# Moving a sum of weights ahead of its operand, and three operand loads ahead of a store, in the second MLP product of an encoder block

## The chip, the cores and the metric

The kernel runs on one core of one Trainium2 chip. The metric is the device time of one execution in microseconds (us), the median over several runs. A core has TensorE (PE, matrix products), VectorE (DVE), ScalarE (ACT), GpSimd (POOL) and SyncE (SP, which here issues the DMAs). Each engine works through its own queue in order; semaphores join them.

## The reference, cut to what matters

One layer of an encoder over 1024 tokens with 1024 channels: attention and a short convolution, gated and merged, then the squared-ReLU MLP that this change lies in:

```python
h = rms_norm(x, norm2_g) @ w_mlp_in          # 1024 -> 4096
x = x + jnp.square(jax.nn.relu(h)) @ w_mlp_out   # 4096 -> 1024
```

Inputs and outputs are float32.

## The kernel before, in words

Float32 products are made from float16 pairs: each operand is scaled by a power of two and split into a high and a low half (the high half by ACT, the low half by VectorE as the scaled value less the high half), and three of the four products of halves are summed (`PASSES`). Large products are also done by a scheme of Strassen's kind: the matrices are cut into 2 x 2 blocks, and seven products of sums of blocks take the place of eight.

**First MLP product.** It runs in 16 quads, `q` = 0 to 15 (`quad`, `seven`). A quad has seven units of 12 matmuls, in the order 1, 6, 5, 4, 2, 7, 3, with an evacuation ("post") for each: `post5`, `post7` (L1298 to L1300) and `post3` (L1303) on VectorE, and others on L1295, L1307, L1308 and L1310. When a quad is done, `h_done(q)` lets ACT take the ReLU and the square (L1269, L1271), lets POOL make the sums of blocks (L1138) and stores all seven forms to HBM, in `HS[q // 4]` (L1275, on SP). So HS[0] holds quads 0 to 3, and HS[3] is complete with quad 15.

**Second MLP product.** It sums over four sections `s` of the hidden channels. A section has seven products `o` = 0 to 6 in the order of `ORDER`: w11, t2, w21, t3, t1, t4, w22. That is 28 groups, n = 7 s + o, of four units each (`j`, one for every 128 tokens of a block); a unit is 12 matmuls and fills one bank. Weights of the section are `w11`, `w12` (four raw tiles) and `w21`, `w22` (tile w2x); sums of them are made in place by POOL: after w11's operand is ready, w11 becomes t1 = w11 + w12 (L1403) and t2 = w11 + w12 + w22 is written to a tile of its own (L1404); after t2's, w12 becomes w12 + w22 = t3 (L1408); after t3's, t2 takes up w21 and so becomes t4 (L1412).

`prep2(s)` prepares a section's operands. It squares the weights on ACT into a scratch tile, keeping only the sums of squares (L1357, L1360); from these it gets a scale, through a column sum on VectorE and TensorE (`sum_of`, L924, and `scale_of`, which waits for three units of matmuls). Then for each group it scales and splits the activations (ACT L1388, VectorE L1390) and the weights (ACT L1393, VectorE L1397, two halves each) into the tile `OPS[16 + n]`. These tiles rotate through three buffers (`TAGS`), and `gate(i)` holds a group back until TensorE's instructions of two groups ahead of it have been issued; the buffer itself comes free when TensorE has read it. Activations come back from HS by `h_load(n)` (L1343) into one of four slots of the tile `hf`, slot n % 4. Two are loaded apart: n = 0 into half of the tile h0 (L1426), and n = 1 into that half of `OPS[17]` where its weights will later stand (L1368). So L1393 of n = 1 can write only when L1390 of n = 1 has read. For section 0 the other half of h0 is first the scratch for squares and then the tile of t2; later sections have the tiles `junk` and `t2`.

The order of instructions is made by generators. Each `unit` emits its matmuls, then the post of the unit ahead (`settle`), and then lets foreground generators take `steps` steps and the first background generator (`prep2` at the end of the kernel) `ticks` ticks up to its next `yield`. So where a `yield` stands sets the place of an instruction in its engine's queue. During quad 15, n = 0's and n = 1's operands are prepared between its posts. `hf` lies in the buffer of u2T, the activations of the first product, so `h_load(2)` comes after quad 15; `h_load(3)` is issued when all stores of sums have been issued:

```python
    h_load(2)
    settle()
    while live:
        step()
    h_load(3)
```

After that, group n issues `h_load(n + 2)`. Posts of the second product add a bank into `acc` (ACT L1487 for s = 0, VectorE L1489 later) or straight into the residual `X1` (VectorE L1498). In the last section `combine` (L1460 to L1469) adds the accumulators on POOL and VectorE, and finished rows are stored.

Of the kernel before, what the change touches and what calls it, by code (L numbers as in the profile page):

```python
# [11 lines left out]
F16 = mybir.dt.float16  # L12
BF16 = mybir.dt.bfloat16
I32 = mybir.dt.int32
AF = mybir.ActivationFunctionType
OP = mybir.AluOpType
# [36 lines left out]
def encoder_block(ctx: ExitStack, tc: tile.TileContext, x, weights, cols, gqk, rel, masks, out):  # L53
    nc = tc.nc
    V, A, G, T, SP = nc.vector, nc.scalar, nc.gpsimd, nc.tensor, nc.sync
# [27 lines left out]
    def cols_of(kind, n):  # L83
        a = area[kind]
        if a[1] + n > a[2]:
            assert kind != "keep"
            a[1] = a[0]
        a[1] += n
        return slice(a[1] - n, a[1])

    def keep(n=1):
        return cols_of("keep", n)
# [4 lines left out]
    def at(c, i, n=1):  # L97
        return slice(c.start + i, c.start + i + n)

    def mul(a, b, out=None):  # L100
        out = out or tmp(a.stop - a.start)
        V.tensor_tensor(sc[:, out], sc[:, a], sc[:, b], op=OP.mult)
        return out
# [23 lines left out]
    def step(n=1):  # L127
        for _ in range(n):
            for g in list(fg):
                if not advance(g):  # L130
                    fg.remove(g)
# [42 lines left out]
    def ones_col():  # L174
        turn[0] = (turn[0] + 1) % 4
        return ones[:, 128 + turn[0]:129 + turn[0]]
# [23 lines left out]
    def settle():  # L200
        while late:
            late.pop(0)()
# [9 lines left out]
    def load_upto(n):  # L212
        while loaded[0] < min(n, len(loads)):
            ch, p = loads[loaded[0]]
            loaded[0] += 1
            t = rawp.tile([128, 1024], F32, name="raw")
            load_into(t[:, :ch.widths[p][0] * ch.widths[p][1]], ch, p)
            ch.raw.append(t)
# [637 lines left out]
    for k in range(N + 11):  # L856
        p, w = k // 16, k % 16
# [63 lines left out]
    def sum_of(sm):  # L921

        b, a = cols_of("prep", 1), ones_col()
        V.tensor_reduce(sc[:, b], sc[:, sm], axis=AX, op=OP.add)  # L924
        V.tensor_copy(a, sc[:, b])
        return a, work[0]

    def scale_of(am, more, n=3):

        a, mark = am  # L930
        yield from apart(mark, n * 6144, work)
        b, s, inv = cols_of("prep", 1), cols_of("prep", 1), keep()
        yield from all_sum(a, b, anybank(), 1e-36)
        yield from pow2_half(b, 14, s, inv, more)
        return s, inv
# [239 lines left out]
    TAGS = ((base2, "B"), (base, "K"), (base, "V"))  # L1175
    tsum = {}

    def gate(i):
        while pe_done[0] < i - 2 or (i == 2 and pair_done[0] < 4):
            yield  # L1180
# [54 lines left out]
    def wait(n):  # L1235
        for _ in range(n):
            yield
# [93 lines left out]
    OPS, X2 = {}, {}  # L1331
    later = {}

    def w2x_load(s):
        pool = later["pool"] if s == 1 else wsp
        X2[s] = pool.tile([128, 4, 1024], F32, name="w2x", tag="w2x" if s == 1 else "ws", bufs=1 if s == 1 else 2)
        for i in range(4):
            load_into(X2[s][:, i], c2x[s], i)

    def h_load(n):  # L1340
        s, f = n // 7, ORDER[n % 7][0]
        later["h", n] = later["hf"][:, n % 4]
        SP.dma_start(later["h", n], HS[s][:, f])  # L1343
# [3 lines left out]
    def prep2(s):  # L1347
        raw, x2 = c2[s].raw, X2[s]
        w11, w12 = raw[0:2], raw[2:4]
        w21, w22 = [x2[:, i] for i in range(2)], [x2[:, i] for i in range(2, 4)]  # L1350
        while not r_ready[s]:
            yield
        Rs, iR = R[s]
        sm = cols_of("prep", 6)
        j = later["junk"]
        for i in range(4):
            A.activation(j[:, :1024], raw[i], AF.Square, scale=sc[:, iR], accum_out=sc[:, at(sm, i)])  # L1357
            yield
        for i in range(2):
            A.activation(j, x2[:, 2 * i:2 * i + 2].rearrange("p a c -> p (a c)"), AF.Square, scale=sc[:, iR],  # L1360
                         accum_out=sc[:, at(sm, 4 + i)])
            yield
        sums = sum_of(sm)
        if s == 0:
            yield from gate(17)
            P = OPS[17] = TAGS[17 % 3][0].tile([128, 2, 2, 2048], F16, name="ops", tag=TAGS[17 % 3][1])
            later["h", 1] = P[:, 0].rearrange("p w m -> p (w m)").bitcast(F32).rearrange("p (k t) -> p k t", k=4)
            SP.dma_start(later["h", 1], HS[0][:, ORDER[1][0]])  # L1368
        sw, inv = yield from scale_of(sums, 0)
        fw = keep()  # L1370
        mul(iR, sw, fw)
        c2[s].inv = inv
        yield
        T2 = None
        for o, (f, name) in enumerate(ORDER):
            n = 7 * s + o
            i = 16 + n
            yield from gate(i)
            pool, tag = TAGS[i % 3]
            if n != 1:  # L1380
                OPS[i] = pool.tile([128, 2, 2, 2048], F16, name="ops", tag=tag)
            P = OPS[i]
            while ("h", n) not in later:
                yield
            if 1 < n < 26:
                h_load(n + 2)
            hf = later.pop(("h", n)).rearrange("p k t -> p (k t)")
            A.activation(P[:, 1, 0], hf, AF.Copy, scale=sc[:, Rs])  # L1388
            yield
            V.scalar_tensor_tensor(P[:, 1, 1], hf, sc[:, Rs], P[:, 1, 0], op0=OP.mult, op1=OP.subtract)  # L1390
            w = {"w11": w11, "t1": w11, "t3": w12, "w21": w21, "w22": w22}.get(name) or [T2[:, i] for i in range(2)]
            for i2 in range(2):
                A.activation(P[:, 0, 0, 1024 * i2:1024 * i2 + 1024], w[i2], AF.Copy, scale=sc[:, fw])  # L1393
            yield
            for i2 in range(2):
                sl = slice(1024 * i2, 1024 * i2 + 1024)
                V.scalar_tensor_tensor(P[:, 0, 1, sl], w[i2], sc[:, fw], P[:, 0, 0, sl], op0=OP.mult, op1=OP.subtract)  # L1397
                yield
            ready.add(i)
            if name == "w11":  # L1400
                T2 = later["t2"]()
                for i2 in range(2):
                    G.tensor_tensor(w11[i2], w11[i2], w12[i2], op=OP.add)  # L1403
                    G.tensor_tensor(T2[:, i2], w11[i2], w22[i2], op=OP.add)  # L1404
                    yield
            elif name == "t2":
                for i2 in range(2):
                    G.tensor_tensor(w12[i2], w12[i2], w22[i2], op=OP.add)  # L1408
                yield
            elif name == "t3":  # L1410
                for i2 in range(2):
                    G.tensor_tensor(T2[:, i2], T2[:, i2], w21[i2], op=OP.add)  # L1412
                yield
            elif name == "t1":
                done[0] += 4
                load_upto(done[0] + 5)
                if s < 3:
                    w2x_load(s + 1)
                    bg.append(prep2(s + 1))
            yield  # L1420

    def first2():
        h0 = wsp.tile([128, 2, 4, 512], F32, name="h0", tag="ws")
        w2x_load(0)
        later["h", 0] = h0[:, 0]
        SP.dma_start(h0[:, 0], HS[0][:, 0])  # L1426
        later["t2"] = lambda: h0[:, 1].rearrange("p (a k) t -> p a (k t)", a=2)
        later["junk"] = h0[:, 1].rearrange("p k t -> p (k t)").bitcast(BF16)[:, :2048]
        yield from wait(12)

    bg.append(first2())
    bg.append(prep2(0))
    whole(14)
    whole(15)


    later["hf"] = base.tile([128, 4, 4, 512], F32, name="hf", tag="U")
    h_load(2)
    settle()
    while live:  # L1440
        step()
    h_load(3)
    p4.close()
    p5 = ExitStack()
    w5p = later["pool"] = p5.enter_context(tc.tile_pool(name="p5", bufs=1, reuse_waits="tile"))
# [1 line left out]
    t2 = w5p.tile([128, 2, 1024], F32, name="t2")  # L1447
# [25 lines left out]
    for n in range(28):  # L1473
        s, o = n // 7, n % 7
# [92 lines left out]
```

## Time and profile before

| | |
|---|---|
| median of 3 runs | 1295.95 us (1295.22 to 1296.48) |
| the profiled execution, own time | 1298.12 us |
| its span, first to last instruction | 1296.0 us |
| granted TensorE clock over the span | 0.981 of full |
| busy: PE / DVE / ACT / POOL | 94% / 73% / 59% / 33% |
| second MLP product on TensorE | from 976.9 us to the end |

Times in the profile are us from the start of the span. A line such as L1397 is a line of the kernel. In a timeline a row gives the start, the length, the engine, the line, the operation, output <- input, shape and count; a bracket at its end holds the idle time of the engine just before it and what ended that idle time. Matmuls are pipelined, so a unit's row is a little longer than the distance to the next one.

### The profile page before, as it was taken

The numbers are of one execution on the slowest core, as the hardware profiler recorded it, in microseconds if no ns is written. First come the engines' busy times: TensorE is split into PE (matmuls) and PEld (weight loads), VectorE is DVE, ScalarE is ACT, GpSimd is POOL, SyncE is SP. The second block draws the span as 40 slices with busy tenths as digits, with TensorE's granted clock in tenths as the row PEclk, the third lists the DMA queues.
The fourth block names the chain that finished last, engine by engine and source line by source line (L and its number), as shares of the span: only waits on it lengthen the run. The fifth ranks groups of instructions, "written<-read, shape, count | busy, mean of one in ns | idle before, by whom it ended". The sixth has DMA issues, their size and how long they took to land. (4 is left out here: it accounts for less than half of the span.)

```text
span 1296.0 us, 17018 instructions
## 1 busy us (share of the span) xinstructions
PE 1217.8 (94%) x6294; PEld 579.5 (45%) x6294; DVE 940.0 (73%) x1719; ACT 763.9 (59%) x1169; POOL 433.7 (33%) x269
## 2 busy tenths in 40 slices
PE   5999997889999999999997899999996899999998
PEld 4544443444444444444456444444442344444443
DVE  7578767878657686886575476667746588889798
ACT  6777557667564455533665678777774564646430
POOL 2430011111231111100102587667738316080562
PEclk8999999989999999999998999999998899999999
DMA  6558445646552221225284454445462762526112
GB/s 251 125 196 159 106 70 118 132 81 139 113 112 84 65 65 37 70 86 193 63 165 104 147 179 140 151 157 179 170 228 90 240 239 92 234 98 244 67 64 98
DMA packets 170803, 173.35 MB, mean 134 GB/s; under 512 B 131424, under 2 KB 131936, under 8 KB 166624
## 3 DMA queue, kind: packets, MB, share of 16 engines
q1 hardware_dynamic: 170720, 172.27, 44.8%
q8 instruction: 49, 0.80, 0.3%
q14 instruction: 34, 0.28, 0.1%
HBM read 102.51 MB, written 37.75 MB: 108 GB/s over the span
## 5 line engine op out<-in xcount | busy, mean ns | idle before, releaser
L188 PEld LDWEIGHTS <-w 128*128 128x128 f16 x1512 | 149.7, 100 | 161.8 <-issue 9.8
L188 PEld LDWEIGHTS <-ops 128*128 128x128 f16 x1356 | 133.5, 99 | 181.3 <-issue 26.7
L1138 POOL TENSOR_TENSOR as<-as 128x512 f32<-128x512 f32 x64 | 111.7, 1746 | 85.3 <-ACT as L1271 81.6
L854 PE MATMUL ps_d<-uT,w_ws 128*128 128x512 f16 x528 | 128.3, 384 | 2.5 <-ACT w_ws L290 2.4
L188 PE MATMUL ps_s<-ops 128*128 128x512 f16 (+1 forms) x528 | 121.3, 380 | 7.1 <-ACT acc L1487 4.2
L188 PE MATMUL ps_d<-ops 128*128 128x512 f16 x492 | 115.4, 385 | 9.7 <-DVE as L1298 9.7
L188 PEld LDWEIGHTS <-uT 128*128 128x128 f16 x648 | 64.7, 100 | 70.7 <-issue 5.9
L1388 ACT ACTIVATE ops<-hf,sc 128x2048 f16<-128x2048 f32 x26 | 51.8, 1994 | 69.7 <-PE ps_d L188 24.7
L188 PE MATMUL ps_d<-u2T,w 128*128 128x512 f16 (+1 forms) x420 | 89.4, 365 | 3.3 <-DMA u2T<-v 2.9
L971 DVE SCALAR_TENSOR_TENSOR w<-raw,sc,w 128x512 f16<-128x512 f32 (+1 forms) x32 | 40.7, 1272 | 67.7 <-ACT w L977 67.7
L188 PEld LDWEIGHTS <-w_s 128*128 128x128 f16 x588 | 56.7, 98 | 71.3 <-DMA uT<-gs 2.2
L188 PE MATMUL ps_s<-u2x,w 128*128 128x512 f16 (+1 forms) x396 | 85.1, 366 | 3.2 <-DMA u2x<-v 3.2
L1390 DVE SCALAR_TENSOR_TENSOR ops<-hf,sc,ops 128x2048 f16<-128x2048 f32 x26 | 70.7, 2718 | 16.0 <-ACT ops L1388 16.0
L944 ACT ACTIVATE raw<-raw,sc 128x256 f32<-128x256 f32 x184 | 76.0, 494 | 6.1 <-DMA raw<-in_weights 6.1
L188 PE MATMUL ps_o<-ops 128*128 128x512 f16 x336 | 77.5, 380 | 1.4 <-DVE ops L1397 0.8
L958 POOL TENSOR_TENSOR tsum<-raw 128x512 f32<-128x512 f32 x30 | 50.8, 1710 | 81.2 <-ACT raw L944 66.3
L854 PEld LDWEIGHTS <-w_ws 128*128 128x128 f16 x528 | 51.1, 99 | 58.3 <-issue 3.9
L1403 POOL TENSOR_TENSOR raw<-raw 128x1024 f32<-128x1024 f32 x8 | 22.7, 2837 | 140.8 <-DVE ops L1397 140.8
L1269 ACT ACTIVATE as<-as 128x2048 f32<-128x2048 f32 x16 | 30.5, 1909 | 62.9 <-DVE as L1303 62.9
L958 POOL TENSOR_TENSOR gsum<-raw 128x512 f32<-128x512 f32 x14 | 18.5, 1338 | 133.4 <-issue 68.7
L971 DVE SCALAR_TENSOR_TENSOR w<-tsum,sc,w 128x1024 f16<-128x1024 f32 x30 | 61.4, 2087 | 0.0
L278 DVE SCALAR_TENSOR_TENSOR w_ws<-raw,sc,w_ws 128x512 f16<-128x512 f32 (+2 forms) x72 | 51.1, 764 | 3.5 <-ACT w_ws L290 3.5
(300 smaller groups left out, 2526.4 us busy)
## 6 DMA issues: line engine op xcount, KB each, us to landing
raw<-in_weights SPq DMA_DIRECT2D x92, 512.0 KB, 4.0
hs<-as SPq DMA_DIRECT2D x16, 1792.0 KB, 6.9
hf<-hs SPq DMA_DIRECT2D x26, 1024.0 KB, 10.4
w2x<-in_weights SPq DMA_DIRECT2D x16, 512.0 KB, 6.8
raw<-in_weights SPq DMA_DIRECT2D x16, 384.0 KB, 4.0
xt<-in_x SPq DMA_DIRECT2D x8, 512.0 KB, 9.8
gs<-s SPq DMA_DIRECT2D x4, 1024.0 KB, 6.6
x<-in_x SPq DMA_DIRECT2D x8, 512.0 KB, 8.6
```

Source lines behind the costliest of these rows:

```text
L188: T.matmul(ps, l, r, start=a, stop=b)
L278: V.scalar_tensor_tensor(lo, self.raw[p][:, o:o + m], sc[:, c:c + 1], hi, op0=OP.mult, op1=OP.subtract)
L854: T.matmul(ps, l, r, start=a, stop=b)
L944: A.activation(v, v, AF.Copy, scale=sc[:, at(g, 4 * i + k)])
L958: G.tensor_tensor(t[:, o], a, b, op=OP.add)
L971: V.scalar_tensor_tensor(P[:, a:b, 1], w, sc[:, s], P[:, a:b, 0], op0=OP.mult, op1=OP.subtract)
L1138: sub.tensor_tensor(z[o], z[a], z[b], op=op)
L1269: A.activation(f[:, 0:4], f[:, 0:4], AF.Relu)
L1388: A.activation(P[:, 1, 0], hf, AF.Copy, scale=sc[:, Rs])
L1390: V.scalar_tensor_tensor(P[:, 1, 1], hf, sc[:, Rs], P[:, 1, 0], op0=OP.mult, op1=OP.subtract)
L1403: G.tensor_tensor(w11[i2], w11[i2], w12[i2], op=OP.add)
```

## The change

In section 0 the scratch for the squares is no longer half of h0 but part of `OPS[16]`, the operand tile of n = 0, which is therefore taken earlier (behind `gate(16)`). In all sections t2 is made on POOL right behind the squares, as w12 + w22 and then + w11, which are four POOL additions; behind w11's operand only the two that make t1 remain. The yields there change with it: one behind the new additions, one behind t1's instead of two. `h_load(2)`, `h_load(3)` and `h_load(4)` are issued together ahead of the last store of sums, and group n issues `h_load(n + 3)` instead of `h_load(n + 2)`.

```diff
@@ prep2
-        j = later["junk"]
+        if s == 0:
+            yield from gate(16)
+            OPS[16] = TAGS[16 % 3][0].tile([128, 2, 2, 2048], F16, name="ops", tag=TAGS[16 % 3][1])
+            j = OPS[16][:, 0, 0].bitcast(BF16)
+        else:
+            j = later["junk"]
...
         sums = sum_of(sm)
+        T2 = later["t2"]()
+        for i in range(2):
+            G.tensor_tensor(T2[:, i], w12[i], w22[i], op=OP.add)
+            G.tensor_tensor(T2[:, i], T2[:, i], w11[i], op=OP.add)
+        yield
...
-        T2 = None
...
-            if n != 1:
+            if n > 1:
                 OPS[i] = pool.tile([128, 2, 2, 2048], F16, name="ops", tag=tag)
...
-            if 1 < n < 26:
-                h_load(n + 2)
+            if 1 < n < 25:
+                h_load(n + 3)
...
             if name == "w11":
-                T2 = later["t2"]()
                 for i2 in range(2):
                     G.tensor_tensor(w11[i2], w11[i2], w12[i2], op=OP.add)
-                    G.tensor_tensor(T2[:, i2], w11[i2], w22[i2], op=OP.add)
-                    yield
+                yield
@@ first2
-        later["junk"] = h0[:, 1].rearrange("p k t -> p (k t)").bitcast(BF16)[:, :2048]
@@ behind quad 15
-    h_load(2)
+    for n in (2, 3, 4):
+        h_load(n)
     settle()
     while live:
         step()
-    h_load(3)
```

## The prediction

> **What bounds the kernel now.** I read the page first, then TensorE's timeline from the first unit of the second MLP product (group n = 0, where its operands are named ops) to the end, and behind each gap the other engines' timelines and the waits.
>
> ```profile
> span 1296.0 us, 17018 instructions
> PE 1217.8 (94%) x6294; PEld 579.5 (45%) x6294; DVE 940.0 (73%) x1719; ACT 763.9 (59%) x1169; POOL 433.7 (33%) x269
> ```
>
> TensorE is busy 94% of the span, so a change to the preparation of operands can only be worth what TensorE idles, or runs at a low clock, in the stage it touches. All edits lie in that product, so the gaps there are the whole budget.
>
> ```profile
> 976.86 1.73 PE L188 MATMUL ps_o<-ops 128*128 128x512 f16 x7
> ...
> 980.41 2.75 PE L188 MATMUL ps_d<-ops 128*128 128x512 f16 x12
> 983.00 2.75 PE L188 MATMUL ps_s<-ops 128*128 128x512 f16 x12
> ...
> 995.48 5.28 PE L188 MATMUL ps_d<-ops 128*128 128x512 f16 x12 [9.72 <-DVE as L1298]
> 1003.48 2.75 PE L188 MATMUL ps_o<-ops 128*128 128x512 f16 x12
> ...
> 1019.02 2.75 PE L188 MATMUL ps_d<-ops 128*128 128x512 f16 x12
> 1025.94 0.59 PE L188 MATMUL ps_s<-ops 128*128 128x512 f16 x1 [4.16 <-ACT acc L1487]
> ...
> 1034.33 2.75 PE L188 MATMUL ps_d<-ops 128*128 128x512 f16 x12
> ...
> 1092.10 2.75 PE L188 MATMUL ps_o<-ops 128*128 128x512 f16 x12 [0.60 <-DVE acc L1489]
> ...
> 1258.73 2.75 PE L188 MATMUL ps_s<-ops 128*128 128x512 f16 x12 [0.47 <-DVE x L1498]
> ...
> 1281.67 2.75 PE L188 MATMUL ps_s<-ops 128*128 128x512 f16 x12 [2.06 <-DVE x L1498]
> ...
> 1289.44 2.78 PE L188 MATMUL ps_s<-ops 128*128 128x256 f16 x24
> ```
>
> Each row is one unit of 12 matmuls: start, length, and in brackets the idle time before it with its releaser. Three undisturbed units separate the last two rows: 7.77 / 3 = 2.59 us a unit. The 112 units (28 groups of 4) would take 290.1; from 976.86 to 1289.44 + 2.59 they take 315.2. So 25.1 us are lost, and the rows hold nearly all of it:
> - start of n = 0: 980.41 - 976.86 - 2.59 = 0.96;
> - first large gap, with the slow units after it: 1003.48 - 983.00 - 3 x 2.59 = 12.7 (9.9 of gap, 2.8 of low clock);
> - second large gap: 1034.33 - 1019.02 - 3 x 2.59 = 7.5;
> - the three late ones: 0.60 + 0.47 + 2.06 = 3.1.
>
> The other 0.8 I leave alone.
>
> **The first gap** is told by three engines together.
>
> ```profile
> 969.93 8.28 POOL L1138 TENSOR_TENSOR as<-as 128x512 f32<-128x512 f32 x4 [17.48 <-ACT as L1271]
> ...
> 988.24 3.20 POOL L1404 TENSOR_TENSOR h<-raw,w2x 128x1024 f32<-128x1024 f32 x1
> ...
> 991.47 1.15 ACT L1393 ACTIVATE ops<-h,sc 128x1024 f16<-128x1024 f32 x1 [4.43 <-POOL h L1404]
> ...
> 979.21 4.43 DVE L1390 SCALAR_TENSOR_TENSOR ops<-ops,sc 128x2048 f16<-128x2048 f32 x1
> ...
> 987.07 2.17 DVE L1397 SCALAR_TENSOR_TENSOR ops<-h,sc,ops 128x1024 f16<-128x1024 f32 x1 [2.83 <-ACT ops L1393]
> 992.65 2.17 DVE L1397 SCALAR_TENSOR_TENSOR ops<-h,sc,ops 128x1024 f16<-128x1024 f32 x1 [3.41 <-ACT ops L1393]
> 994.75 0.68 DVE L1298 TENSOR_TENSOR as<-ps_d,as 128x512 f32<-128x512 f32 x1
> ```
>
> POOL finishes t2 (tile h) only at 991.4: it first does the sums of quad 14, then adds w11 and t2 in turn. ACT's copy for n = 1 waits, VectorE's L1397 waits behind it, and behind L1397 in VectorE's queue stands L1298, which reads the bank that TensorE needs for the fourth unit of n = 0. So TensorE restarts at 995.48.
>
> **Edit 1, t2 behind the squares.** It takes two POOL adds a section from behind w11's operand and puts four ahead (two adds for each of two halves): two more a section. POOL idles 17.48 us before 969.93. t2's buffer is not a scratch for squares any more (n = 0's own tile is) and w12, w22 are all it needs. A 128x1024 add takes:
>
> ```profile
> L1403 POOL TENSOR_TENSOR raw<-raw x8: 2342/2838/3329, 978.2 to 1216.8; 128x1024 f32<-128x1024 f32 x8
> w2x<-in_weights SPq DMA_DIRECT2D x4, 512.0 KB, 5.7
> 949.57 1.88 SPq L210 DMA_DIRECT2D w2x<-in_weights  x4
> ```
>
> The last w2x is issued at about 951.0 and lands 5.7 later, 956.7. Four adds of 2.34 to 3.33 end at 966 to 970, hidden in the idle stretch. If they run late, the sums of quad 14 are queued behind them (due 967 to 970), and behind these the store and the loads.
>
> The new scratch tile also lets the squares start sooner.
>
> ```profile
> 947.04 2.18 ACT L977 ACTIVATE w<-tsum,sc 128x1024 f16<-128x1024 f32 x2
> 953.57 1.15 ACT L1357 ACTIVATE h<-raw,sc 128x1024 bf16<-128x1024 f32 x1 [4.35 <-DVE w L971]
> 958.66 2.00 ACT L1360 ACTIVATE h<-w2x,sc 128x2048 bf16<-128x2048 f32 x1
> 962.92 0.16 DVE L924 TENSOR_REDUCE sc<-sc 128x1 f32<-128x6 f32 x1 [7.39 <-ACT h L1360]
> ```
>
> ACT waited 4.35 for VectorE to leave that buffer. The new scratch lies in a buffer that quad 13 read last, two quads earlier, so ACT can begin at 949.3, do the four raw squares in 5.1 and the w2x pair (4.2) when it has landed, about 955.7: end near 960 instead of 962.9. I take 2.5 us earlier (bounds 0, if landing is late, and 4.35). VectorE stood 7.39 us at L924, with quad 14's posts queued behind it, so its whole queue moves.
>
> New course: L1390 of n = 1 started at 979.21, right behind n = 0's last L1397; it now starts at 976.7, so n = 0 is ready when TensorE asks for it at 976.86 (0.96 saved). At 4.43, as POOL will again be adding, it ends at 981.1; its f32 source lies where L1393 writes, so ACT waits for it, then copies the first half, 1.15; L1397 2.17, L1310 (a PSUM post like L1298, now between the halves, since w11 yields once less) 0.68, L1397 2.17, L1298 0.68: 988.0. TensorE wanted its bank at 985.59, so 2.4 of 9.9 us remain. Fast ends (L1390 2.35, L1397 1.27, in the rows below) give 984.2: no gap; with no advance it is 990.5, a gap of 4.9, with low clock at up to 2.8.
>
> ```profile
> L1390 DVE SCALAR_TENSOR_TENSOR ops<-hf,sc,ops x26: 2332/2352/3789, 1003.3 to 1274.5; 128x2048 f16<-128x2048 f32 x26
> L1397 DVE SCALAR_TENSOR_TENSOR ops<-raw,sc,ops x24: 1268/1277/2301, 974.8 to 1256.7; 128x1024 f16<-128x1024 f32 x24
> 668.00 2.53 PE L188 MATMUL ps_o<-u2T,w 128*128 128x256 f16 x12
> ```
>
> A gap of 2.06 at 1281.67 left the next units at full speed. The row at 668.00, behind a gap of 2.1, took 2.53 for 12 matmuls of 256 columns where the row at 1289.44 has 24 of them in 2.78, so low clock after 2.4 is possible; I take none, keeping 2.8 for the range. [...]
>
> Next late: the operand of n = 2. Quad 15's ACT passes stand before it. L1298 and three posts like it run from 987.3, 0.68 each: 990.0. Then come two ACT passes over 2048 elements and L1388, 2.0 each (the row at 1021.24 below has 2.00), L1390 at 3.0 (an estimate between its 2.35 and 3.79) and two L1397 at 2.17: 1003.3. TensorE is at n = 2 at 988.0 + 12.95 = 1001.0 and needs the second weight half 1.3 later: a wait of 1.0. First gap in all: 12.7 - 2.4 - 1.0 = 9.3 saved.
>
> **Edit 2, loads three ahead.**
>
> ```profile
> hs<-as SPq DMA_DIRECT2D x16, 1792.0 KB, 6.9
> hf<-hs SPq DMA_DIRECT2D x26, 1024.0 KB, 10.4
> ...
> 1009.62 0.53 SPq L1275 DMA_DIRECT2D hs<-as  x1
> ...
> 1021.24 2.00 ACT L1388 ACTIVATE ops<-hf,sc 128x2048 f16<-128x2048 f32 x1 [13.55 <-DMA hf<-hs]
> ```
>
> n = 3's load stood on SP behind the last store, which waits for POOL's sums; it went out behind that store's issue (1009.62 + 0.53) and landed 11 us later, while ACT waited 13.55 and kept the accumulator copies behind it, hence TensorE. Now loads 2, 3, 4 go out behind quad 14's store, at 969.93 + 8.28 - 2.5 = 975.7: 1.8 + 3 x 1.05 MB. They also wait for the buffer of u2T, which quad 15 reads last; TensorE leaves that quad at 976.86. At what the DMA moved when full
>
> ```profile
> 954.00:968.00 14.00, 13.63 (x65) 6.17 (x63) 4.22 (x9) 10.88 (x14) 0.00 (x0) 1.00 1.02 357
> ```
>
> (357 GB/s) that is 14 us: all landed at 991. L1388 wants n = 2 at 994 and n = 3 at about 1000. The last store is behind them on SP and is read only by the fourth section. In steady state a load still waits for its buffer's L1390, four buffers as before: no change. Saved 7.5; if the loads share so badly that n = 3 comes 13 later, 0.
>
> **Edit 3, later sections.** The same t2 wait sits there.
>
> ```profile
> ACT ops L1393 <- POOL t L1404: 36.8, 6, 7.8
> DVE ops L1397 <- ACT ops L1393: 24.8, 8, 3.4
> 1232.48 0.74 DVE L1489 SCALAR_TENSOR_TENSOR acc<-ps_s,sc,acc 128x512 f32<-128x512 f32 x1
> ```
>
> ACT waits 36.8 us for t2 in the three later sections, up to 7.8 at a time. VectorE's row is for all four sections, 24.8 / 8 = 3.1 before each half, 6.2 a section; it then works off sums 13 us late (n = 21's first bank was full at 1258.09 - 16 x 2.59 + 2.59 = 1219.2). That lag causes the 0.60 and, carried on, the 0.47 and 2.06. With t2 ready some 7 us sooner they go: 3.1 (bounds 0 and 3.1).
>
> The sum: 0.96 + 9.3 + 7.5 + 3.1 = 20.9. The profiled execution took 1298.1, its span 1296.0 and 2.1 around it; it becomes 1277.2, and the median of the runs, 2.2 below it, becomes **1275.0**.
>
> **Rivals.**
> B: VectorE's queue beside POOL takes the first gap over: no advance, gap 4.9 plus 2.8 low clock, and half of the late 3.1 kept: 1275.0 + 5.3 + 1.5 = 1282. For it: POOL adds all through 967 to 988.
> C: VectorE is quick there; no gap is left: 1275.0 - 3.4 - 0.8 = 1271.
> D, slower: eight more adds beside VectorE make it the bound. L1390 stretches from 2.35 to 3.79 and L1397 from 1.28 to 2.30 beside POOL, 3.5 us a group. It decides once TensorE waits 7 us more in each of three later sections, the 20.9 over three. Against: VectorE's busy time was 203.0 of 250 us from 1000 to 1250,
>
> ```profile
> 1000.00:1250.00 250.00, 244.86 (x1120) 109.91 (x1119) 202.98 (x196) 134.91 (x124) 101.71 (x36) 0.98 0.43 161
> ```
>
> and gives up the waits for t2. Price at three stretched groups a section: 3 x (10.4 - 7) = 10 over the old time, 1306. [...]
> E: the loads don't help, since bandwidth or ACT's queue keeps n = 3 late: 1275.0 + 7.5 = 1282.5.
>
> **How the numbers follow.** Forecast 0.60, B 0.18, C 0.12, E 0.06, D 0.04. The range runs from 1270.5 (all 25.1 gone, with 0.3 to spare) to 1283, past B and E; 0.2% is 2.6 us, about what a measurement can tell from no change. All but D are faster, even B, E and all of the late 3.1 together (1275.0 + 5.3 + 7.5 + 3.1 = 1291). D in part ends within the bound: faster 0.96, same 0.01, slower 0.03.
>
> **What the profile will show.** Right: POOL adds into h at 956 to 970; ACT's L1393 of n = 1 no longer names POOL; the 9.72 gap shrinks to about 2.4, its releaser still VectorE; ACT never waits for hf; no gap at 1281. Wrong: a gap over 5 us in n = 0 to 2, hf still a releaser, or VectorE gaps behind POOL at the section starts.

## The result, and the profile after

The changed kernel takes 1279.22 us (median of 4 runs, 1277.69 to 1281.09), the kernel before 1296.22 on the same chip (4 runs). The ratio is 0.9867, 95% interval 0.9849 to 0.9886. The profiled execution took 1279.16 us, its span is 1277.0. In the new source L1388 has become L1397, L1390 L1399, L1393 L1402, L1397 L1406, L1487 L1493, L1489 L1495 and L1498 L1504; the additions for t2 are L1371 and L1372.

TensorE's timeline of the second product, as before:

```profile
975.49 2.75 PE L188 MATMUL ps_o<-ops 128*128 128x512 f16 x12
...
980.67 2.75 PE L188 MATMUL ps_s<-ops 128*128 128x512 f16 x12
987.75 5.28 PE L188 MATMUL ps_d<-ops 128*128 128x512 f16 x12 [4.32 <-DVE as L1298]
992.82 3.21 PE L188 MATMUL ps_s<-ops 128*128 128x512 f16 x12
995.87 2.75 PE L188 MATMUL ps_o<-ops 128*128 128x512 f16 x12
...
1270.48 2.78 PE L188 MATMUL ps_s<-ops 128*128 128x256 f16 x24
```

One gap is left. From 975.49 to 1270.48 + 2.59 the 112 units take 297.6 us, 7.5 more than 112 x 2.59 where it was 25.1 before. Nearly all of the 7.5 is this gap and the slow units behind it: 987.75 - 980.67 - 2.59 = 4.5, and 995.87 - 987.75 - 2 x 2.59 = 2.9. So 17.6 us went inside the product. Another 1.4 lies ahead of it (it begins at 975.49 instead of 976.86): 0.4 is the wait at 963.91, which is gone, and most of the rest (0.9) was already there when quad 14 began, ahead of everything that the change touches. Together that is the span's 19.0. The medians of the runs differ by 17.0 only, since the profiled execution of before lies 1.9 us above its median (1298.12 against 1296.22) and that of the changed kernel lies on its own median.

POOL, ACT and VectorE around the gap that is left (each engine's timeline):

```profile
956.11 2.35 POOL L1371 TENSOR_TENSOR h<-raw,w2x 128x1024 f32<-128x1024 f32 x1 [4.51 <-issue]
...
963.30 2.35 POOL L1372 TENSOR_TENSOR h<-h,raw 128x1024 f32<-128x1024 f32 x1
966.50 7.38 POOL L1138 TENSOR_TENSOR as<-as 128x512 f32<-128x512 f32 x4 [0.85 <-ACT as L1271]
975.05 7.68 POOL L1411 TENSOR_TENSOR raw<-raw 128x1024 f32<-128x1024 f32 x2 [1.17 <-DVE ops L1406]
982.69 6.61 POOL L1415 TENSOR_TENSOR raw<-raw,w2x 128x1024 f32<-128x1024 f32 x2
...
980.61 2.19 ACT L1402 ACTIVATE ops<-h,sc 128x1024 f16<-128x1024 f32 x2 [6.01 <-DVE ops L1399]
...
976.09 4.43 DVE L1399 SCALAR_TENSOR_TENSOR ops<-ops,sc 128x2048 f16<-128x2048 f32 x1
981.79 2.02 DVE L1406 SCALAR_TENSOR_TENSOR ops<-h,sc,ops 128x1024 f16<-128x1024 f32 x1 [1.28 <-ACT ops L1402]
...
984.34 2.76 DVE L1406 SCALAR_TENSOR_TENSOR ops<-h,sc,ops 128x1024 f16<-128x1024 f32 x1
987.02 0.68 DVE L1298 TENSOR_TENSOR as<-ps_d,as 128x512 f32<-128x512 f32 x1
```

t2 is finished at 965.65, in POOL's idle stretch, at 2.35 an addition. ACT's copy for n = 1 no longer waits for POOL but for VectorE's L1399, whose float32 source lies where the copy writes. L1399 takes 4.43 and the two halves of L1406 2.02 and 2.76, while POOL makes t1 (L1411, 975.05 to 982.7) and then t3 (L1415) beside them.

The loads, on SP and at ACT's activation scaling of n = 3, which waited 13.55 us before and now has no bracket:

```profile
974.52 3.02 SPq L1343 DMA_DIRECT2D hf<-hs  x3
...
999.84 2.00 ACT L1397 ACTIVATE ops<-hf,sc 128x2048 f16<-128x2048 f32 x1
```

In the last section VectorE adds n = 21's first bank at 1211.77. TensorE had filled it at 1270.48 - 27 x 2.59 + 2.59 = 1203.1, so VectorE is 8.6 us behind where it was 13 before. The gaps at n = 9, 25 and 27 are gone.

```profile
1211.77 0.74 DVE L1495 SCALAR_TENSOR_TENSOR acc<-ps_s,sc,acc 128x512 f32<-128x512 f32 x1
```

### The profile page after: what moved, and what is told of

Same layout as the page of the kernel before. It is cut to its first block, busy times and chain, and to the rows that moved or that the text cites. A ratio compares the mean times of both kernels' runs of the same rounds, so it can differ in the third digit from the quotient of the medians.

```text
span 1277.0 us, 17035 instructions
## 1 busy us (share of the span) xinstructions
PE 1214.9 (95%) x6294; PEld 578.5 (45%) x6294; DVE 961.3 (75%) x1719; ACT 763.7 (60%) x1169; POOL 463.0 (36%) x277
## 4 chain that ended last, share of the span: by engine, by line
PE 66%; DVE 15%; ACT 8%; DMA 5%; issue 4%; POOL 2%; SPq 1%; DVEq 0%; ACTq 0%; POOLq 0%
PE ps_d L188 24%; PE ps_s L188 22%; PE ps_o L188 14%; PE ps_d L854 5%; DMA PT<-P 2%; DMA hs<-as 2%; DVE w_s L971 1%; DVE w_ws L278 1%; ACT w L977 1%; POOL sform L480 1%; PE ps_s L778 1%; PE ps_o L835 1%; DVE sz L792 1%; DVE sc L301 1%; ACT raw L944 1%
## 5 line engine op out<-in xcount | busy, mean ns | idle before, releaser
L188 PE MATMUL ps_s<-ops 128*128 128x512 f16 (+1 forms) x528 | 118.7, 375 | 0.0
L1397 ACT ACTIVATE ops<-hf,sc 128x2048 f16<-128x2048 f32 x26 | 52.0, 1999 | 95.1 <-PE ps_d L188 39.9
L1399 DVE SCALAR_TENSOR_TENSOR ops<-hf,sc,ops 128x2048 f16<-128x2048 f32 x26 | 72.3, 2781 | 7.3 <-ACT ops L1397 7.3
L290 ACT ACTIVATE w_ws<-raw,sc 128x512 f16<-128x512 f32 (+2 forms) x72 | 40.9, 636 | 20.0 <-DVE sc L253 20.0
```

What stands on the lines that cost most here:

```text
L188: T.matmul(ps, l, r, start=a, stop=b)
L290: A.activation(self.parts[:, 0, f + o:f + o + m], self.raw[p][:, o:o + m], AF.Copy, scale=sc[:, c:c + 1])
```

## The experiments

In each, one code edit is told against the kernel named. The kernel before ran with them on the same chips, at medians of 1296.95 to 1297.26 us; ratios are to it.

### 1. t2 alone

The changed kernel with the loads put back:

```diff
-            if 1 < n < 25:
-                h_load(n + 3)
+            if 1 < n < 26:
+                h_load(n + 2)
...
-    for n in (2, 3, 4):
-        h_load(n)
+    h_load(2)
     settle()
     while live:
         step()
+    h_load(3)
```

> t2 made behind the squares as in the changed kernel, loads two ahead and n = 3's load behind the last store, as before. Chain theory: the first gap is the changed kernel's (4.3 us and 2.9 of low clock) and the late gaps are gone; the last store goes out at about 1002 instead of 1009.6, so n = 3's load lands at about 1012 and TensorE, 4.7 us behind the landing as before, waits about 3.5 us at n = 3, with up to 2.9 of low clock: 1283 to 1286 us. Rival, each edit is worth its own gap of before whatever the other does: 1279.2 + 7.5 = 1286.7. Rival, the loads are worth nothing once t2 is early: 1279.

Measured: 1288.44 us, ratio 0.9934 (0.9917 to 0.9951); the profile's span is 1284.2. In this section and the next ones "product" is the stretch from TensorE's first unit of n = 0 to its last unit. ACT's and TensorE's timelines:

```profile
1012.59 2.00 ACT L1397 ACTIVATE ops<-hf,sc 128x2048 f16<-128x2048 f32 x1 [12.62 <-DMA hf<-hs]
...
1017.29 0.59 PE L188 MATMUL ps_s<-ops 128*128 128x512 f16 x1 [3.53 <-ACT acc L1493]
1018.22 4.85 PE L188 MATMUL ps_s<-ops 128*128 128x512 f16 x11 [0.35 <-DVE ops L1406]
```

The landing near 1012, the 4.7 us from it to TensorE and the gap of 3.5 came as the chain says; the late gaps are gone. The low clock behind the gap (4.85 for 11 matmuls) makes it cost 7.1 us, nearly the 7.5 that it cost before. The first gap was 4.93 here, not the 4.3 that was expected. By time alone the chain and the rival "each edit is worth its own gap" are not told apart here, and the median lies over both; the gap and the landing speak for the chain. That the loads are worth nothing once t2 is early has fallen.

### 2. The loads alone

The kernel before with the loads of the changed one (the diff of 1 the other way round).

> Loads three ahead and ahead of the last store; t2 made behind w11's operand, as before. Chain theory: the gap of 9.7 us at n = 0 and its low clock stay, the gap at n = 3 (7.5 with low clock) goes, the late gaps stay: 1288 to 1290 us. Rival, the t2 wait of the later sections fills what the loads free, as ACT and VectorE now come to it with less lead: 1291 to 1294 us, with late gaps larger than 3.1.

Measured: 1290.97 us, ratio 0.9955 (0.9939 to 0.9971), span 1288.7.

```profile
997.13 4.10 PE L188 MATMUL ps_d<-ops 128*128 128x512 f16 x12 [9.71 <-DVE as L1298]
...
1084.74 2.75 PE L188 MATMUL ps_o<-ops 128*128 128x512 f16 x12 [0.60 <-DVE acc L1489]
...
1251.41 2.75 PE L188 MATMUL ps_s<-ops 128*128 128x512 f16 x12 [0.50 <-DVE x L1498]
...
1274.36 2.75 PE L188 MATMUL ps_s<-ops 128*128 128x512 f16 x12 [2.06 <-DVE x L1498]
```

The gap at n = 3 is gone, the first gap and the three late ones stand unchanged (9.71, 0.60, 0.50, 2.06). The median lies 1 us past the range of the chain theory, at the edge of the rival's; what decides is that the late gaps did not grow, so the rival has fallen.

### 3. t2 early in sections 1 to 3 only

The kernel before, with the four additions behind the squares where `s` is not 0.

```diff
         sums = sum_of(sm)
+        if s:
+            T2 = later["t2"]()
+            for i in range(2):
+                G.tensor_tensor(T2[:, i], w12[i], w22[i], op=OP.add)
+                G.tensor_tensor(T2[:, i], T2[:, i], w11[i], op=OP.add)
+            yield
```

> t2 behind the squares in sections 1 to 3 only; section 0 and the loads as before. Chain theory: only the gaps at n = 9, 25 and 27 go, 3.1 us: 1293 us, and VectorE no longer waits behind ACT's copy of t2 in these sections. Rival, the late gaps come from VectorE working beside POOL in the last section and not from the wait for t2: 1296 us, with the gap at the last group still there.

Measured: 1292.68 us, ratio 0.9971 (0.9958 to 0.9984), as the chain gave. No gap at n = 9, 25 or 27 is left. The profiled execution's product is 3.0 us shorter than before. In ACT's waits (us in total, times, longest; L1400 and L1395 are the weight and the activation scaling of this source), the one of 36.8 us for the later sections' t2 is gone and that of section 0 stays:

```profile
ACT ops L1400 <- POOL h L1413: 13.6, 2, 9.2
ACT ops L1395 <- DMA hf<-hs: 13.6, 1, 13.6
```

So the late gaps came from the wait for t2, though VectorE works beside POOL in the last section as before (POOL is busy for 46.9 of the 80 us from 1190, 43.8 before).

### 4. Fewer sums, and none beside VectorE at n = 1

The changed kernel with the sums in another order: w12 becomes w12 + w22 (which is t3) at once, t2 is w11 + that, and t1 is t2 - w22, made two operands later. Eight POOL operations a section instead of ten.

```diff
         for i in range(2):
-            G.tensor_tensor(T2[:, i], w12[i], w22[i], op=OP.add)
-            G.tensor_tensor(T2[:, i], T2[:, i], w11[i], op=OP.add)
+            G.tensor_tensor(w12[i], w12[i], w22[i], op=OP.add)
+            G.tensor_tensor(T2[:, i], w11[i], w12[i], op=OP.add)
...
             if name == "w11":
-                for i2 in range(2):
-                    G.tensor_tensor(w11[i2], w11[i2], w12[i2], op=OP.add)
                 yield
             elif name == "t2":
-                for i2 in range(2):
-                    G.tensor_tensor(w12[i2], w12[i2], w22[i2], op=OP.add)
+                yield
+            elif name == "w21":
+                for i2 in range(2):
+                    G.tensor_tensor(w11[i2], T2[:, i2], w22[i2], op=OP.subtract)
                 yield
```

> The changed kernel with the sums of weights made in another order: behind the squares w12 becomes w12 + w22 and t2 is w11 + that; t1 is made later, behind w21's operand, as t2 - w22. No POOL addition stands between quad 14's sums and quad 15's. Theory that the remaining gap at n = 0 is VectorE slowed by POOL: L1399 of n = 1 takes 2.35 instead of 4.43 and its two weight halves 1.3 each instead of 2.0 and 2.8, the gap shrinks from 4.3 us to under 1, the low clock behind it (2.9) goes, and the time is 1272 us. Rival, the gap is the length of the chain and not POOL (scale, copies and VectorE's order): these durations stay and the time is 1279 us. Rival, n = 2's operand takes the gap over (its wait behind quad 15's ACT passes): 1275 us with a gap at n = 2.

Measured: 1274.27 us, ratio 0.9831 (0.9813 to 0.9848), span 1269.5. VectorE's, POOL's and TensorE's timelines:

```profile
974.45 2.34 DVE L1399 SCALAR_TENSOR_TENSOR ops<-ops,sc 128x2048 f16<-128x2048 f32 x1
978.06 1.29 DVE L1406 SCALAR_TENSOR_TENSOR ops<-h,sc,ops 128x1024 f16<-128x1024 f32 x1 [1.27 <-ACT ops L1402]
...
987.81 8.11 POOL L1138 TENSOR_TENSOR as<-as 128x512 f32<-128x512 f32 x4 [15.56 <-ACT as L1271]
...
981.80 2.75 PE L188 MATMUL ps_d<-ops 128*128 128x512 f16 x12 [0.42 <-DVE as L1298]
...
997.06 1.24 PE L188 MATMUL ps_o<-ops 128*128 128x512 f16 x5 [0.64 <-DVE ops L1406]
...
1008.01 1.24 PE L188 MATMUL ps_s<-ops 128*128 128x512 f16 x5 [0.43 <-DVE ops L1406]
```

With POOL idle (15.56 us), L1399 takes 2.34 instead of 4.43 and each half of L1406 1.3 instead of 2.0 and 2.8. The gap falls from 4.32 to 0.42, and the unit behind it runs at full speed (2.75; the granted clock was 1.00 from 974 to 990). So the gap that the change leaves was VectorE beside POOL, with its low clock behind it; the chain's length alone was not it. Of the third theory a trace is there: n = 2 waits 0.64 (and n = 3 0.43). Over the whole product 2.0 us are lost, where the changed kernel loses 7.5.

Run again beside the changed kernel on one chip:

> The changed kernel once more, as the partner of the three runs beside it: 1277 to 1281 us, with the one gap of about 4.3 us at n = 0 and some 2.9 us of low clock behind it.

> The version with fewer sums once more, beside the changed kernel on the same chip: the gap at n = 0 stays under 1 us and the time is 6 to 7 us (0.5%) below the changed kernel's. Rival, the difference between the two calls was the chip's: no difference here.

Measured: the changed kernel 1281.14 us, ratio 0.9879 (0.9857 to 0.9901); with fewer sums 1274.98, ratio 0.983 (0.9809 to 0.985). 6.2 us apart, as expected: this version beats both kernels. The two profiled executions of this version differ by 6.3 us in span (1269.5 and 1275.8), but the product loses 2.0 us in the one and 2.6 in the other; it begins at 973.45 and at 979.17. So most of this difference lies ahead of the product, and the length of the product compares these kernels better than a single span does.

### 5. The squares' earlier start

Ahead of section 0's squares ACT writes one element of t2's tile and so waits for VectorE to leave that buffer, as the squares did before.

```diff
             j = OPS[16][:, 0, 0].bitcast(BF16)
+            A.activation(later["t2"]()[:, 0, 0:1], raw[0][:, 0:1], AF.Copy)
```

> The changed kernel, but ahead of section 0's squares ACT writes one element into t2's tile, so that the squares wait again until VectorE has left that buffer, as before the change; t2 stays early. Theory that the earlier squares carry VectorE's whole queue: the column sum L924 is about 2.6 us later, the gap at n = 0 grows by as much, to about 6.9 us, and the time by 2.6. Rival, ACT's and POOL's passes for quad 14 set the queue and the squares' time is hidden: gap and time as in the changed kernel.

Measured: 1280.55 us, ratio 0.9878 (0.9861 to 0.9896), beside the changed kernel's 1281.14 on that chip. The column sum did come later, at 962.24, where the first profile of the changed kernel has it at 959.49. TensorE's timeline:

```profile
963.24 2.75 PE L188 MATMUL ps_d<-u2T,w 128*128 128x512 f16 x12 [0.43 <-DVE as L1298]
978.66 1.24 PE L188 MATMUL ps_o<-ops 128*128 128x512 f16 x5 [0.75 <-DVE ops L1407]
...
990.20 4.61 PE L188 MATMUL ps_d<-ops 128*128 128x512 f16 x12 [5.11 <-DVE as L1298]
```

Of the 2.6 us against that first profile, 1.2 came out as the two small waits ahead of the gap (0.43 and 0.75, as in the kernel before) and only 0.8 in the gap; the unit behind it was slow for less time (4.61 against 5.28). No cost in time is seen. But the changed kernel's own profile on this chip had lost the advance too, which shows how unsure it is: there w2x landed late, and ACT waited for it

```profile
956.11 2.00 ACT L1365 ACTIVATE ops<-w2x,sc 128x2048 bf16<-128x2048 f32 x1 [3.97 <-DMA w2x<-in_weights]
```

where the first profile had 1.51. So its column sum came late as well, and its TensorE shows the same waits and the same gap:

```profile
960.77 0.16 DVE L924 TENSOR_REDUCE sc<-sc 128x1 f32<-128x6 f32 x1 [7.27 <-ACT ops L1365]
...
977.20 1.24 PE L188 MATMUL ps_o<-ops 128*128 128x512 f16 x5 [0.75 <-DVE ops L1406]
...
988.73 4.99 PE L188 MATMUL ps_d<-ops 128*128 128x512 f16 x12 [5.11 <-DVE as L1298]
```

Counted from the start of quad 15, the column sum stands at 4.6 us here (956.16), at 4.8 with the edit (957.44) and at 2.15 in the first profile (957.34). The two profiles from this chip thus hardly differ, and the experiment doesn't show what the earlier squares are worth in the changed kernel; neither theory is settled by it. In the kernel before they are worth 2.4 us (the second run of experiment 7; 0.8 to 3.9 by its interval).

### 6. Two ahead

```diff
-    for n in (2, 3, 4):
+    for n in (2, 3):
...
-            if 1 < n < 25:
-                h_load(n + 3)
+            if 1 < n < 26:
+                h_load(n + 2)
```

> The changed kernel with loads 2 and 3 ahead of the last store and two ahead in the loop, so that load 4 stands behind the last store. Theory that only load 3's place behind the store cost time: load 4 lands near 1012, ACT wanted it at 1006, but TensorE comes to n = 4 only at 1024, so no gap and the changed kernel's time within 1 us. Rival, three ahead is needed: ACT's wait for load 4 holds back the accumulator copies and a gap of 2 us or more appears at n = 3 or 4.

Measured: 1279.31 us, ratio 0.9874 (0.9853 to 0.9896). Load 4 made ACT wait until 1012, and TensorE has no gap there:

```profile
1012.11 2.00 ACT L1397 ACTIVATE ops<-hf,sc 128x2048 f16<-128x2048 f32 x1 [7.24 <-DMA hf<-hs]
```

What counts in the second edit is that load 3 leaves ahead of the last store; the third load ahead is worth nothing measurable.

### 7. POOL as the bound, and the scratch alone

The changed kernel with t2's additions made twice in sections 1 to 3:

```diff
-        for i in range(2):
+        for i in range(2) if s == 0 else (0, 1, 0, 1):
```

> The changed kernel with the four POOL additions of t2 made twice over in sections 1 to 3 (the second time with the same result): about 10 us more of POOL a section, ahead of w11's operand. Theory that VectorE has slack beside POOL there: VectorE's operands of n = 7 and 8 stretch by a few us, TensorE shows no new gap over 1 us, and the time is the changed kernel's within 2 us. Rival of the prediction, POOL's additions beside VectorE make it the bound: TensorE waits 2 us or more in each of the three sections, and the time is 6 us or more above the changed kernel's.

Measured: 1281.99 us, ratio 0.9876 (0.9858 to 0.9894); the changed kernel had 0.9867 and 0.9879 in its own two comparisons. Two small gaps appear, so the slack is not endless:

```profile
1078.01 2.75 PE L188 MATMUL ps_o<-ops 128*128 128x512 f16 x12 [0.85 <-DVE acc L1495]
...
1265.73 2.75 PE L188 MATMUL ps_s<-ops 128*128 128x512 f16 x12 [0.76 <-DVE x L1504]
```

The kernel before with section 0's scratch moved to n = 0's tile and nothing else:

```diff
-        j = later["junk"]
+        if s == 0:
+            yield from gate(16)
+            OPS[16] = TAGS[16 % 3][0].tile([128, 2, 2, 2048], F16, name="ops", tag=TAGS[16 % 3][1])
+            j = OPS[16][:, 0, 0].bitcast(BF16)
+        else:
+            j = later["junk"]
```

> The kernel before with only the scratch moved: section 0's squares go into n = 0's own tile; t2 and the loads as before. Theory that the squares carry VectorE's queue but t2's POOL additions end last: TensorE's waits of 0.37 and 0.75 ahead of the gap go, the squares end about 2.5 us earlier, POOL's sums and so t2 come about 2.5 earlier too, and the gap at n = 0 is 8 to 9 us instead of 9.7: 1293 to 1295 us. Rival, POOL's additions start no earlier: the gap is 10.5 to 11 us, since TensorE comes to it 1.1 us sooner, and the time stays at the kernel before's.

Measured: 1294.55 us, ratio 0.9982 (0.997 to 0.9994). The waits ahead of the gap are gone and the gap is

```profile
992.74 5.00 PE L188 MATMUL ps_d<-ops 128*128 128x512 f16 x12 [9.11 <-DVE as L1298]
```

0.1 over the expected 8 to 9; the time is in the expected range, 2.4 us below the 1296.95 of the kernel before. All of t2 moved with the squares, since POOL's sums of quad 14 stand ahead of it.

## Why the prediction was right, point by point

Forecast 1275.0 in 1270.5 to 1283, measured 1279.2: right in direction, inside the range, 4.2 us too fast. By its steps:

- **The budget** (25.1 us, 24.3 of them in named gaps) held: the span lost what those gaps lost.
- **t2 in POOL's idle stretch**: additions forecast to run to 966 to 970, found from 956.11 to 965.65. Right. ACT's L1402 names VectorE, as forecast.
- **The first gap**: 3.4 us forecast to remain (2.4 of gap, 1.0 at n = 2, no low clock), 7.4 measured (4.5, 0, 2.9). This is the mis-sized term. Three things went into it. First, TensorE's want of the bank was left at 985.59 after its waits of 0.96 and 0.37 ahead of it had been taken away: with them gone it comes 1.3 sooner, and the gap is 1.3 longer. The 0.96 booked as a saving of its own was therefore spent again at the next wait. Second, the chain from L1399 to the end of L1298 took 11.6 us, not 11.3 (a half of L1406 at 2.76, not 2.17), and began 0.3 later relative to quad 15. Third, the low clock was taken as none behind a gap of 2.4; behind 4.3 it cost 2.9. The wait of 1.0 at n = 2 was hidden by that slow clock: without it (experiment 4) n = 2 waits 0.64.
- **How the miss of 4.2 adds up**: that the first gap came out 4.0 dearer is not the whole of it, and that the two numbers nearly agree is chance. In the profile, 0.7 of the 0.8 that had been left alone went too, and 1.4 was gained ahead of the product, so the span was 1277.0 against 1296.0 - 20.9 = 1275.1. The other 2.2 of the miss was the step from the profile to the median: the profile of before was 2.2 above its median, that of the changed kernel lies on its own median.
- **Rival B and luck**: in cost, the first gap came out near B's 4.9 + 2.8 = 7.7, though in the first profile B's condition (no advance) didn't hold. In the second profile of the changed kernel (experiment 5) it did, and the gap of 5.11 is over the 5 us that the prediction named as a sign of being wrong. Of B's price only the late gaps stayed away. So the forecast was right for the loads and the late gaps, and too low for the first gap, where the range and not the forecast covers what came.
- **That VectorE's pace beside POOL would hold what is left**, which the forecast took at 4.43 and rival B named, is shown by experiment 4: without POOL beside it 0.42 of the gap of 4.32 is left.
- **The loads**: 7.5 forecast, the gap is gone. Right, and experiment 6 shows that its cause was the place behind the store.
- **The late gaps**: 3.1 forecast, all gone, and experiment 3 shows t2's wait as their cause, at 3.0 us in the product and 4.3 between its medians.
- **The squares 2.5 us earlier**: seen in the first profile (959.49 against 962.92, of which 0.9 is the earlier start of quad 15), lost in another execution where w2x landed late, the lower bound that was given. In the kernel before it is worth 2.4 us (experiment 7); its worth in the changed kernel is not shown.
- **Rivals**: C fell with the 4.5 that remained; D fell with experiment 7; E fell with the profile, where ACT never waits for hf.

Nearly settled: whether the two main edits overlap in worth. Alone their ratios give 0.66% and 0.45%, together 1.33%, and the intervals allow both a sum and a little more or less. In the profiles the product is 9.9 us shorter with t2 alone, 9.0 with the loads alone, and 17.6 (in the second profile 16.5) with both: close to a sum, with an overlap of one or two us at most.

## What to carry to other kernels

When a wait is taken away, move the time at which the next wait is wanted as well: savings on the same engine ahead of a later gap only lengthen that gap (here by 1.3 us). A sum that an idle engine can make early should go where that engine is idle and also where the other engine's operations are not slowed by it (here L1399 took 4.43 us beside POOL's additions for t1 and 2.34 with POOL idle); algebra (t1 as t2 - w22) may free the place. A load must leave ahead of a store that waits for late work (here ACT waited 13.55 us for one behind such a store); how many loads ahead matters less (here 1279.31 us with two and 1281.14 with three, on one chip).

## What the runs showed of the hardware

VectorE's L1399 of n = 1 and POOL's additions for t1 took longer side by side than alone, in all nearly as long as one after the other. Two additions of 128x1024, 2.35 each alone (956.11), took 7.68 beside L1399; L1399 took 4.43, and 2.34 with POOL idle (experiment 4). Their times alone, 4.7 + 2.3, come to 7.0, nearly the 7.7 in which POOL made its two. One by one:

```profile
975.05 3.32 POOL L1411 TENSOR_TENSOR raw<-raw 128x1024 f32<-128x1024 f32 x1 [1.17 <-DVE ops L1406]
976.09 4.43 DVE L1399 SCALAR_TENSOR_TENSOR ops<-ops,sc 128x2048 f16<-128x2048 f32 x1
978.33 4.40 POOL L1411 TENSOR_TENSOR raw<-raw 128x1024 f32<-128x1024 f32 x1
```

These rows fit turns, in which the one that starts second waits until the other has ended. That is an estimate from the times alone: L1399's 4.43 would be 2.1 of waiting, until the first addition is done near 978.3, and 2.34 of its own; the second addition's 4.40 would be 2.05 of waiting, until L1399 is done at 980.5, and 2.35 of its own. (The first addition's 3.32 would likewise hold 1.0 of waiting, behind a half of L1406.) What makes either wait is not shown. Two of VectorE's posts, which read a bank, took 0.68 beside POOL's L1415 (L1310 at 983.74 and L1298 at 987.02), as L1298 did in the kernel before at 963.18, with POOL idle.

The gap of 4.3 us on TensorE was followed by 2.9 us lost to a low clock (the granted clock was 0.50 from 987.75 to 993.0), one of 0.42 by none. The loss did not grow with the gap: it was 2.2 and 1.9 behind the two gaps of 5.11 in experiment 5, 2.3 behind the 9.11 of experiment 7, 1.4 behind the 9.71 of experiment 2 and 2.8 behind the 9.72 of the kernel before. So these gaps cost their own length and 1.4 to 2.9 us on top. Near 2 us it went both ways in the kernel before: behind the 2.06 at 1281.67 the granted clock was 1.00, behind the 2.09 that ends at 666.08 it was 0.53 from 668.0 to 670.3.
